# A hybrid decoder trunk: the first mixer's output projection as seven block products

## The chip, the core and the metric

The kernel runs on one core of one Trainium2 chip, in one launch. The metric is the device time of one execution in microseconds (us). A core has five engines that run their own instruction streams and wait for each other by semaphores: TensorE (PE) multiplies matrices into PSUM banks, VectorE (DVE) and GpSimd (POOL) do elementwise work, ScalarE (ACT) casts and activates, and SyncE (SP) issues the DMAs. In this kernel all DMAs of weights and activations are issued on SP's queue, in one order.

## The reference, cut to what matters

x is 1 x 1024 x 1024 (tokens by channels), float32. Layer 0 mixes by a gated delta rule (mixer A, 4 heads of 128) and a short gated convolution (mixer B, 512 channels); layer 1 has other mixers. Each mixer's outputs are concatenated and mapped by one output projection; a SwiGLU FFN follows each.

```
def mixer_ab(...):
    ...
    return jnp.concatenate([o_a, o_b], axis=-1) @ w_out          # 1024x1024 by 1024x1024

def reference(x, ...):
    h = x
    for layer in range(DEPTH):                                   # DEPTH = 2
        hn = rms_norm(h, norm_mix_g[layer])
        h = h + (mixer_ab if layer % 2 == 0 else mixer_cd)(hn, ...)
        hn = rms_norm(h, norm_ffn_g[layer])
        h = h + swiglu(hn, ffn_w_gate[layer], ffn_w_up[layer], ffn_w_down[layer])
    return rms_norm(h, norm_final_g)
```

The case is about `concat @ w_out` of layer 0, the addition to h behind it and the `rms_norm` that follows.

## The kernel before

Activations are kept transposed: channels on the 128 partitions, tokens along the free axis, in two halves of 512 tokens (`NH` = 2, `HT` = 512) and eight blocks of 128 channels (`KT` = 8, `KH` = 4). Precision is kept by splitting: `split(hi, lo, src)` lets ACT cast a float32 tile to a shorter type (L102) and DVE subtract that from it (L103), and `mm3` multiplies a 128x128 block of weights with a 128x512 block of activations by three matmuls, hi x hi, hi x lo and lo x hi (L127, L128, L129). A weight unit is one 128x1024 tile, loaded by one 512 KB DMA into `raw` (tag "raw", 2 buffers) and split into `w` (`unit()`, 4 buffers).

*The mixer's front.* `mixer_ab` opens with a loop over four heads and two halves (`for u in range(8)`, L1606). Each turn makes q, k, v and the gate z by projections on PE, runs a causal convolution over them on DVE (`xp` L1315, `cacc` L1531 and L1533), and lets `step(u, i)` work on the scalars and the chunk matrices of an earlier turn (`cx`, L1570 to L1589). POOL does little there: copies and clears of the convolution's carry (L1312, L1314, L1524), one 128x512 mask product a turn (L1589), and the power that makes an inverse root (`pow`: `power` L216 for the trunk's norm, L1559 for q and k). The norm of the second half of x is made inside the first turns: `sums` (PE L200, then DVE `rows` L204), `inverse` (PE transposes the rows, L209; DVE copies `v`, L211; POOL raises it to -1/2, L216) and `spread` (PE L240 copies the result over the partitions). `bat` (L1332, PE L1338) carries the decay and write-strength columns to the scalars `s_g` (PE L1435, L1436).

*The order.* The program's tiles and pools decide the buffers; a scheduler puts each engine's instructions in an order by priorities and a cost model, so that an instruction's place on its engine can differ from its place in the source. SP's and POOL's orders are fixed once built: what stands behind a waiting instruction waits with it.

*The output projection.* `out_proj` (L1265) runs once for each half of the tokens. It loads the eight 128x512 blocks of the concatenated mixer outputs (`cat`, in DRAM) into `cin`, splits them (`hnh`, `hnl`), and for each of eight blocks of output channels multiplies eight blocks of weights: 2 x 8 x 8 x 3 = 384 matmuls, into `psu` and `psg` banks. Each result is added to the residual tile of h by DVE (L1282); `tr.piece` squares it on ACT (L181, L184) and gathers the squares on POOL (`acc`, L188), and `tr.save` stores it to DRAM (L244). The residual itself was loaded by `tr.begin` (L168). While the second half's blocks run, the norm of the first half is made: `tr.sums` after block d = 1, `tr.inverse` after d = 2 and `norm_first` (L271) after d = 3, which spreads the norm (L240), scales eight tiles of h (DVE) and splits them. Behind it comes the FFN: `Up.turn` (L617 to L628) loads its first weights (`raw` L626, L627), makes sums of weights on POOL (`Up.sums`, L327 and L328; L617), and starts with `p1(0, b11)` and the second half's norm, `tr.sums(1)`. The FFN already uses seven block products for each of its pairs (`p1` to `p7`).

Of the kernel before, what the change touches and what calls it, by code (L numbers as in the profile page):

```python
# [9 lines left out]
F32 = mybir.dt.float32  # L10
# [8 lines left out]
P = 128  # L19
# [36 lines left out]
def hybrid_trunk_kernel(ctx: ExitStack, tc: tile.TileContext, x_t, w_all, w_down, w_ba, vecs, c_f, c_i, c_rope, out):  # L56
# [1228 lines left out]
                yield  # L1285


    def mixer_ab(hn, rb, hp, tr, first, later, second, close, wba):
        scr_n = dr.tile([4, 32, 32, 32], F32, name="scr_n")
        scr_y = dr.tile([4, 32, 32, 32], F32, name="scr_y")  # L1290
        scr_c = dr.tile([8, P, 4, CX], F32, name="scr_c")
# [99 lines left out]
        with ExitStack() as es:  # L1391
# [121 lines left out]
            if True:  # L1513
# [92 lines left out]
                for u in range(8):  # L1606
                    h, half = divmod(u, 2)
                    if half == 0:
                        wqk, wvz = first if h == 0 else (wload(("ab", h), ("ab", 4 + h)),
                                                         wload(("ab", 8 + h), ("ab", 12 + h)))  # L1610
                        carry = at("carry", (3, 3), p=fp)
                    kk = at("kq", (2, HT), 3, fp)
                    v = at("vch", p=fp)
                    conv_silu(h, 0, wk(wqk, 0), half, carry, kk[:, 1, :])
                    step(u, 0)
                    conv_silu(h, 1, wk(wqk, 1), half, carry, kk[:, 0, :])
                    step(u, 1)
                    conv_silu(h, 2, wk(wvz, 0), half, carry, v)
                    step(u, 2)
                    z_gate(h, half, wk(wvz, 1), early.pop((u, 3), None))  # L1620
                    step(u, 3)
                    waiting.append((h, half, kk, v))
            def inverses():
# [883 lines left out]
    for layer in range(2):  # L2507

        if layer == 0:
            mixer_ab(hn, rb, hp, tr, first, later, second, es.close, wba)  # L2510
# [12 lines left out]
        row = R_FFN + layer * KT  # L2523
        for half in range(NH):
            steps = out_proj(("abo", "cdo")[layer], cat[layer][half], tr, residual[half],
                             ((4, 5, 6, 7, 0, 1, 2, 3), (0, 1, 2, 4, 5, 6, 3, 7))[layer], half, hp)
            for d, _ in enumerate(steps):
# [118 lines left out]
```

## Time and profile before

| what | us |
|---|---|
| median of 3 runs | 2542.97 (2541.15 to 2545.13) |
| the profiled execution's own time | 2541.42 |
| its span | 2539.6 |
| PE busy in it | 2513.7 |
| DVE busy | 1695.1 |
| ACT busy | 1079.6 |
| POOL busy | 644.3 |

The span runs from the first to the last instruction; 1.8 us of the execution lie outside it. Times in rows of the timeline count from the span's start. A row of the timeline gives start, duration, engine, line, operation, written tile and read tiles, shape and type, count, and in brackets the idle time of the engine ahead of it with what ended that. A row of the stretches gives its bounds and length, then the busy time (and the number of instructions) of PE, PE's weight loads, DVE, ACT and POOL, the granted clock, DMA's share and GB/s. A row of the waits names the waiting engine, tile and line, the releaser, and the sum, number and longest of the waits. Rows of DMA issues end with KB and the median us to landing. Matmuls are pipelined, so a matmul's row lasts longer than the step from one start to the next.

### The profile page before, as it was taken

To read this page: it belongs to the slowest core of one execution; us is meant where nothing else is said; L and a number is where in the kernel's file an instruction comes from. 1 tells how busy PE (TensorE), PEld (TensorE's weight loads), DVE (VectorE), ACT (ScalarE), POOL (GpSimd) and SP (SyncE) were. 2 spreads that over 40 slices of the span, in tenths; PEclk is the share of its full clock that TensorE was granted. 3 is DMA by queue.
4 is the path that set the end of the run, shared out by engine and by line. 5 is a ranking of instruction groups with operands and counts; after the bars stand their busy time and mean duration, and the time that the engine had idled before them with its cause. 6 is when DMAs were issued, how large, how long until landed. Compare 5 with 4: busy or idle time off the path is not lost.

```text
span 2539.6 us, 37517 instructions
## 1 busy us (share of the span) xinstructions
PE 2513.7 (99%) x13957; PEld 2083.5 (82%) x13957; DVE 1695.1 (67%) x2857; ACT 1079.6 (43%) x1827; POOL 644.3 (25%) x557
## 2 busy tenths in 40 slices
PE   9999999999999999999999999999999999999998
PEld 7888888888888888878887889888788888888887
DVE  8887786685656565567788666567668565666554
ACT  5432113353333345334676544456535333334442
POOL 0111111343333300033566410000133333330001
PEclk9999999999999999999999999999999999999999
DMA  4435447325556688544344534576732555568753
GB/s 161 156 121 167 128 155 260 114 92 182 182 191 210 204 299 295 182 139 141 127 141 147 191 120 135 156 199 213 245 137 87 177 190 191 200 216 286 276 175 125
DMA packets 281174, 451.48 MB, mean 178 GB/s; under 512 B 49152, under 2 KB 137760, under 8 KB 280736
## 3 DMA queue, kind: packets, MB, share of 16 engines
q1 hardware_dynamic: 280992, 449.10, 53.8%
q8 instruction: 109, 1.79, 0.3%
q14 instruction: 73, 0.60, 0.1%
HBM read 304.74 MB, written 144.26 MB: 177 GB/s over the span
## 4 chain that ended last, share of the span: by engine, by line
PE 38%; DVE 5%; ACT 3%; issue 2%; POOL 1%; DMA 1%; SPq 0%; POOLq 0%; DVEq 0%; ACTq 0%
PE psu L127 7%; PE psu L129 7%; PE psu L128 7%; PE psg L127 3%; PE psg L128 3%; PE psg L129 3%; PE psm L127 2%; PE psm L129 2%; PE psm L128 2%; PE psm L2255 1%; ACT w L102 1%; DVE w L103 1%; PE psg L1985 0%; POOL sw L853 0%; DVE c L832 0%
## 5 line engine op out<-in xcount | busy, mean ns | idle before, releaser
L103 DVE TENSOR_TENSOR w<-raw,w 128x1024 fp32r<-128x1024 f32 (+1 forms) x322 | 385.1, 1198 | 122.0 <-ACT w L102 121.4
L102 ACT CAST w<-raw 128x1024 fp32r<-128x1024 f32 (+1 forms) x322 | 307.9, 958 | 267.1 <-PE psu L129 135.6
L127 PE MATMUL psu<-hnh,w 128*128 128x512 f32 x832 | 331.7, 399 | 0.5 <-ACT w L102 0.5
L129 PE MATMUL psu<-hnh,w 128*128 128x512 f32 x832 | 325.8, 392 | 0.5 <-DVE w L103 0.5
L128 PE MATMUL psu<-hnl,w 128*128 128x512 f32 x832 | 325.2, 391 | 0.0
L188 POOL TENSOR_TENSOR acc<-acc,sq 128x512 f32<-128x512 f32 x52 | 78.7, 1514 | 517.0 <-ACT sq L184 477.3
L129 PEld LDWEIGHTS psu<-hnh,w 128*128 128x128 f32 x832 | 156.6, 188 | 34.6 <-DVE w L103 0.8
L127 PEld LDWEIGHTS psu<-hnh,w 128*128 128x128 f32 x832 | 156.7, 188 | 33.0 <-ACT w L102 1.0
L128 PEld LDWEIGHTS psu<-hnl,w 128*128 128x128 f32 x832 | 156.7, 188 | 31.0
L327 POOL TENSOR_TENSOR ws<-raw 128x512 f32<-128x512 f32 x54 | 70.5, 1306 | 400.6 <-DMA raw<-in_dram 201.6
L103 DVE TENSOR_TENSOR w<-ws,w 128x1024 fp32r<-128x1024 f32 x51 | 67.1, 1317 | 117.3 <-ACT w L102 117.3
L103 DVE TENSOR_TENSOR hidq<-hr,hidq 128x1024 fp32r<-128x1024 f32 x72 | 82.1, 1141 | 78.7 <-ACT hidq L102 78.7
L102 ACT CAST hidq<-hr 128x1024 fp32r<-128x1024 f32 x72 | 70.3, 980 | 103.3 <-DMA hr<-ts 60.3
L127 PE MATMUL psm<-hidq,w 128*128 128x512 f32 (+1 forms) x275 | 106.1, 386 | 0.0
L128 PE MATMUL psm<-hidq,w 128*128 128x512 f32 (+1 forms) x275 | 105.8, 385 | 0.0
L129 PE MATMUL psm<-hidq,w 128*128 128x512 f32 (+1 forms) x275 | 105.8, 385 | 0.0
L853 POOL TENSOR_TENSOR sw<-sw,rope 128x512 f32<-128x512 f32 x48 | 71.6, 1491 | 96.0 <-ACT sw L852 62.7
L127 PE MATMUL psu<-t3h,w 128*128 128x512 f32 x240 | 93.8, 391 | 1.4 <-ACT u L390 1.4
L127 PE MATMUL psu<-t4h,w 128*128 128x512 f32 x240 | 93.7, 391 | 0.5 <-ACT c L397 0.5
L418 POOL TENSOR_TENSOR hid<-hid,c 128x512 f32<-128x512 f32 x44 | 62.0, 1410 | 126.5 <-ACT hid L417 126.4
L333 POOL TENSOR_TENSOR raw<-raw,ws 128x512 f32<-128x512 f32 x51 | 77.9, 1528 | 62.5 <-DVE w L103 62.5
L128 PE MATMUL psu<-t4l,w 128*128 128x512 f32 x240 | 93.4, 389 | 0.0
(536 smaller groups left out, 6684.1 us busy)
## 6 DMA issues: line engine op xcount, KB each, us to landing
raw<-in_dram SPq DMA_DIRECT2D x227, 512.0 KB, 4.2
sd<-in_dram SPq DMA_DIRECT2D x44, 512.0 KB, 3.9
hid<-hid SPq DMA_DIRECT2D x88, 256.0 KB, 2.9
sd<-sd SPq DMA_DIRECT2D x44, 512.0 KB, 3.3
hr<-ts SPq DMA_DIRECT2D x40, 512.0 KB, 4.4
raw<-sd SPq DMA_DIRECT2D x40, 512.0 KB, 4.6
qk<-z SPq DMA_DIRECT2D x52, 256.0 KB, 2.9
hd<-h SPq DMA_DIRECT2D x48, 256.0 KB, 2.4
```

The costliest lines, as they stand in the source:

```text
L102: S.copy(hi, src)
L103: eng.tensor_tensor(lo, src, hi.bitcast(F32), op=SUB)
L127: T.matmul(o, lh, rh, start=first and i == 0, stop=False, **kw)
L128: T.matmul(o, lh, rl, start=False, stop=False, **kw)
L129: T.matmul(o, ll, rh, start=False, stop=last and i == n - 1, **kw)
L188: (eng or G).tensor_tensor(a, a, q, op=ADD)
L327: G.tensor_tensor(s[:, HT:], b[:, :HT], b[:, HT:], op=ADD)
L333: G.tensor_tensor(a[:, HT:], a[:, HT:], s[:, :HT], op=SUB)
L418: G.tensor_tensor(h, h, self.c22.pop(f), op=MULT)
L853: G.tensor_tensor(sw, sw, self.table[:, 1, t], op=MULT)
L2255: T.matmul(po[:, jj * P:(jj + 1) * P], pt[:, z.start + i * P:z.start + (i + 1) * P], self.vp[:, j - m + 1 + i, :], start=i == 0, stop=i == ...
```

## The change

The projection of layer 0 is made over both halves of the tokens at once, as a product of 2 x 2 blocks: output channels and input channels in halves of 512, tokens in halves of 512. Seven products of 512x512 by 512x512 take the place of eight, by sums on both sides. With x = the operand's upper channels of token half 0, z its lower channels, y and w the same of token half 1:

- the operands' sums are t1 to t4, made from x, y, z, w in place: y - w (t3) and then x + y - w (t2) on DVE, z less t2 (t4) and w less t2 (t1) on POOL, two operations of 128x1024 each;
- the weights' sums are four matrices of 512x512. They are made in the mixer's front by POOL (`sums`, four 128x512 operations for each of four pairs of output blocks), from a 1 MB tile `cin` filled by two 512 KB loads (`load`), and written to DRAM by one 1 MB store into `so`; the projection reads them from there as weight units;
- the seven products run one after another, each over four blocks of output channels (`q`), on two sets of four PSUM banks, `oa` and `ob`; three of them are accumulated onto what stands in `oa`, one onto what stands in `ob`, and after each block DVE adds the bank into a tile of h (28 adds);
- the residual is loaded in four lots between the products; the first half's norm is made inside the sixth product (`tr.sums` after q = 0, `tr.inverse` after q = 1, `norm_first` after q = 2);
- PE's order within this stage is written out by hand (`manual_schedule` for PE); the other engines' orders and everything outside are the scheduler's.

In the built order the first `load` stands behind the mixer's first weight load on SP, the first `sums` follow the first three copies of the carry on POOL (in the profile of before at 29.69), the other three come between there and about 90 us. Layer 1's projection is left as it was. `quarter()` gives a 128x4x512 pair of hi and lo; `tag="m"` of `hp` was four buffers of 128x512 and is one of 128x4x512.

```
+    class Seven:
+        def __init__(self, name, hp):
+            self.name, self.hp = name, hp
+            self.sums_d = dr.tile([4, P, KH, HT], F32, name="so")
+            self.block = None
+        def place(self):
+            return self.hp.tile([P, KH, HT], F32, tag="m", name="cin", bufs=1)
+        def load(self, q):
+            a = self.place()
+            for i in range(2):
+                dma(a[:, 2 * i:2 * i + 2, :], w_all[W_AT[self.name, q + i * KH]].rearrange("p (x c) -> p x c", x=2))
+            self.block = q, a
+        def sums(self):
+            q, a = self.block
+            a12, a11, a22, a21 = (a[:, i, :] for i in range(4))
+            G.tensor_tensor(a22, a21, a22, op=ADD)
+            G.tensor_tensor(a21, a11, a21, op=SUB)
+            G.tensor_tensor(a11, a22, a11, op=SUB)
+            G.tensor_tensor(a12, a12, a11, op=SUB)
+            dma(self.sums_d[:, :, q, :].rearrange("s p n -> p s n"), a)
+        def weights(self, src):
+            us = []
+            for g in range(2):
+                t = ring.tile([P, DM], F32, tag="raw", name="raw", bufs=2)
+                if isinstance(src, int):
+                    dma(t, self.sums_d[src][:, 2 * g:2 * g + 2, :].rearrange("p i c -> p (i c)"))
+                else:
...
+                us.append(unit())
+                split(us[-1][:, 0, :], us[-1][:, 1, :], t)
+            return us
+        def run(self, cat_d, tr, src, row):
...
+            def part(o, us, b, q, first):
+                u, c = us[q // 2], q % 2 * HT
+                mm3(o, [(u[:, 0, c + k * P:c + (k + 1) * P], u[:, 1, c + k * P:c + (k + 1) * P], b[0][:, k, :],
+                         b[1][:, k, :]) for k in range(KH)], first, True, skip_group_check=True)
+            def add(half, d, o, done=False):
+                h = tr.at(half, d)
+                V.tensor_tensor(h, h, o, op=ADD)
+                if done:
+                    tr.piece(half, d, n=(d + half * KH) % KT)
+                    tr.save(half, d, hd[0][half])
+            def each(op, eng, dst, x, y):
+                for a in (0, 2):
+                    eng.tensor_tensor(dst[:, a:a + 2, :], x[:, a:a + 2, :], y[:, a:a + 2, :], op=op)
...
+                b11, b21 = quarter(), quarter()
+                splits(b11, x)
+                w1 = self.weights((0, hi))
+                operand(z, 0, lo)
+                splits(b21, z)
+                w2 = self.weights((0, lo))
+                operand(y, 1, hi)
+                operand(w, 1, lo)
...
+                w6 = self.weights(1)
+                tr.load(0, src[0], range(KH))
+                oa = [psg(), psm(), psm(), psm()]
+                ob = [psu(), psu(), psu(), psg()]
+                for q in range(4):
+                    part(oa[q], w1, b11, q, True)
+                    add(0, q, oa[q])
+                each(SUB, V, y, w, y)
+                each(ADD, V, x, y, x)
+                t2 = quarter()
+                splits(t2, x)
+                w7 = self.weights(3)
+                tr.load(1, src[1], range(KH))
+                for q in range(4):
+                    part(ob[q], w2, b21, q, True)
+                    add(0, q, ob[q], True)
+                t3 = quarter()
+                splits(t3, y)
+                each(SUB, G, z, z, x)
...
+                for q in range(4):
+                    part(oa[q], w6, t2, q, False)
+                    add(1, q, oa[q])
+                t4 = quarter()
+                splits(t4, z)
+                each(SUB, G, x, w, x)
+                w4 = self.weights((1, lo))
...
+                for q in range(4):
+                    part(oa[q], w7, t3, q, False)
+                    add(1, q + KH, oa[q])
+                t1 = quarter()
+                splits(t1, x)
+                w5 = self.weights(2)
+                for q in range(4):
+                    part(oa[q], w4, t4, q, False)
+                    add(0, q + KH, oa[q], True)
+                b22 = quarter()
+                splits(b22, w)
+                w3 = self.weights(0)
+                for q in range(4):
+                    part(ob[q], w5, t1, q, True)
+                    add(1, q + KH, ob[q], True)
+                    if q == 0:
+                        parts = tr.sums(0, ahead=60)
+                    if q == 1:
+                        dg = tr.inverse(*parts)
+                    if q == 2:
+                        first = norm_first(tr, row, dg)
+                for q in range(4):
+                    part(ob[q], w3, b22, q, False)
+                    add(1, q, ob[q], True)
+            return first
@@ mixer_ab, the loop over u
                     z_gate(h, half, wk(wvz, 1), early.pop((u, 3), None))
+                    if 2 < u < 7:
+                        seven.sums()
+                    if 1 < u < 6:
+                        seven.load(u - 2)
@@ the loop over the layers
+            seven = Seven("abo", hp)
+            mixer_ab(hn, rb, hp, tr, first, later, second, es.close, wba, seven)
...
-        for half in range(NH):
+        if layer == 0:
+            with tc.manual_schedule(engines={mybir.EngineType.PE}):
+                b1 = seven.run(cat[0], tr, residual, row)
+        for half in range(NH) if layer else ():
```

More of the change, by code (lines that the diff above doesn't have):

```diff
@@ L1289, in mixer_ab @@
+    def mixer_ab(hn, rb, hp, tr, first, later, second, close, wba, seven):
         scr_n = dr.tile([4, 32, 32, 32], F32, name="scr_n")
@@ L2509, in hybrid_trunk_kernel @@
         if layer == 0:
-            mixer_ab(hn, rb, hp, tr, first, later, second, es.close, wba)
+            seven = Seven("abo", hp)
+            mixer_ab(hn, rb, hp, tr, first, later, second, es.close, wba, seven)
         else:
```

18 lines of the change are left out of this document (17 added, 1 removed).

## The prediction

> **What bounds the kernel now.** I read the page's first two parts, then the busy time of each engine by stretches, then what TensorE (PE) waited for, then the timeline of the two stages that the change touches.
>
> ```profile
> span 2539.6 us, 37517 instructions
> PE 2513.7 (99%) x13957; PEld 2083.5 (82%) x13957; DVE 1695.1 (67%) x2857; ACT 1079.6 (43%) x1827; POOL 644.3 (25%) x557
> PEclk9999999999999999999999999999999999999999
> 0.00:60.00 60.00, 57.75 (x287) 41.65 (x288) 49.12 (x83) 33.07 (x50) 6.18 (x19) 1.00 0.46 159
> 60.00:120.00 60.00, 59.01 (x282) 49.24 (x281) 54.08 (x137) 26.40 (x83) 10.74 (x16) 1.00 0.49 157
> 400.00:520.00 120.00, 119.62 (x552) 97.88 (x552) 77.33 (x93) 46.36 (x59) 36.08 (x22) 1.00 0.52 176
> PE psg L1581 <- DVE cx L1586: 1.0, 1, 1.0
> PE psg L129 <- DVE w L314: 0.5, 1, 0.5
> ```
>
> PE is busy 99% of the span at a clock that never falls below the top digit, so a matmul taken away shortens the kernel, and a PE wait that is put in lengthens it; there is nearly no idle time that could swallow one. The stretches (columns: PE, PE loads, DVE, ACT, POOL) show two different surroundings: in the first 120 us VectorE (DVE) is at 82% and 90%, so it has 11 and 6 us of slack and nothing more; in the 120 us round the output projection it has 43. The waits say how near the front already is to DVE: its longest, after the start, is a DVE one.
>
> **What goes: 48 matmuls.**
>
> ```profile
> 408.38 0.40 PE L127 MATMUL psu<-hnh,w 128*128 128x512 f32 x1
> 494.81 0.39 PE L128 MATMUL psg<-hnl,w 128*128 128x512 f32 x1
> 496.40 0.39 PE L129 MATMUL psg<-hnh,w 128*128 128x512 f32 x1
> 496.63 0.39 PE L127 MATMUL psu<-hnh,w 128*128 128x512 f32 x1
> ```
>
> The old projection starts at 408.38 and the FFN's first product at 496.63: 88.2 us for 2 x 8 x 8 x 3 = 384 matmuls and a few small ones. Seven starts lie between 494.81 and 496.40, so one matmul is 1.59/7 = 0.227 us. The new stage has 7 x 4 x 4 x 3 = 336: 48 x 0.227 = **-10.9 us**. The order of PE's instructions really is 48 shorter, so that the change misses its aim altogether is excluded.
>
> **What comes in the front.** Sixteen POOL sums (128x512), eight 512 KB loads and four 1 MB stores. In the source they stand late in the head loop, but in the changed order of POOL the first four follow the carry copy of 29.69 and three of the second block stand ahead of the `pow` of 44.15. On SP each store stands, waiting for its block's last sum, ahead of weight loads; the next two loads, into the same buffer, wait for that store's landing. Rows for this chain:
>
> ```profile
> 29.69 0.19 POOL L1524 COPY carry<-xp 128x3 f32<-128x3 f32 x1 [0.41 <-DVE xp L1315]
> 44.15 1.46 POOL L216 TENSOR_TENSOR r<-v,mhalf 128x4 f32<-128x4 f32 x1
> L188 POOL TENSOR_TENSOR acc<-acc,sq 128x512 f32<-128x512 f32 x52 | 78.7, 1514 | 517.0 <-ACT sq L184 477.3
> scr_c<-cx SPq DMA_DIRECT2D x8, 1216.0 KB, 4.8
> raw<-in_dram SPq DMA_DIRECT2D x227, 512.0 KB, 4.2
> 26.61 0.69 DVE L1315 TENSOR_TENSOR xp<-psu,rb 128x512 f32<-128x512 f32 x1 [0.32 <-ACT rb L1373]
> ...
> 42.92 0.29 DVE L204 TENSOR_SCALAR rows<-psm 128x128 f32<-128x128 f32 x1 [0.66 <-PE psm L200]
> 48.50 0.60 PE L240 MATMUL psm<-cf,r 128*128 128x128 f32 x4
> 50.92 0.68 DVE L1332 TENSOR_TENSOR bat<-psg,rb 128x512 f32<-128x512 f32 x1
> 51.68 0.70 PE L1338 MATMUL psm<-cf,bat 128*128 128x8 f32 x5
> ```
>
> Does a POOL sum cost DVE anything? These rows say yes:
>
> ```profile
> 108.15 0.68 DVE L1315 TENSOR_TENSOR xp<-psu,rb 128x512 f32<-128x512 f32 x1
> 108.37 1.29 POOL L1589 TENSOR_TENSOR cx<-cx,masks 128x512 f32<-128x512 f32 x1 [3.63 <-issue]
> 108.75 1.99 DVE L103 TENSOR_TENSOR w<-raw,w 128x1024 fp32r<-128x1024 f32 x1
> 46.52 1.21 DVE L103 TENSOR_TENSOR w<-raw,w 128x1024 fp32r<-128x1024 f32 x1
> 131.65 1.67 POOL L1589 TENSOR_TENSOR cx<-cx,masks 128x512 f32<-128x512 f32 x1 [3.16 <-DVE cx L1586]
> 132.09 1.91 DVE L1570 SCALAR_TENSOR_TENSOR dm<-bc,s_gc,masks 128x128 f32<-128x128 f32 x3
> 513.44 5.25 POOL L617 TENSOR_TENSOR raw<-xa,raw 128x512 f32<-128x512 f32 x1 [9.23 <-DMA raw<-in_dram]
> 512.91 2.35 DVE L617 TENSOR_TENSOR t1l<-h,t1h 128x1024 fp32r<-128x1024 f32 x2
> ```
>
> The DVE split took 1.21 us at 46.52, but 1.99 at 108.75 beside a POOL operation that ran to 109.66: it lost 0.78. The three small ones at 132.09 met a POOL operation that had 1.23 to run, so lost at most that. The PSUM reader at 108.15 was not slowed. And at 513.44 the loser is POOL: 5.25 us for a 1.3 us operation while DVE streams two-input operations. So a sum costs DVE between 0 and 1.29, mostly about **0.8**, and itself takes 1.3 to 5.3.
>
> [...]
>
> Chain, with 1.51 us a sum (the L188 mean): the first four run 29.9 to 36.0, the store lands at 41, the next loads at 46, three sums end at 50.5, the `pow` at 52.0, where PE wants its result at 48.50: **+3.5**. By then DVE has lost 7 x 0.8 = 5.6, less about 1 of idle time (0.66 at 42.92 and another such gap): `bat` ends 4.6 later and PE at 51.68 with it, **+4.5 in all, not on top**. The two other blocks take 8 x 0.8 = 6.4 from DVE between about 60 and 90 us, of which I let 2.4 go into its gaps (6 us in that whole stretch): +4. Front: **+8.5**. Low end: half the sums fall beside PSUM readers or gaps, 3. High end: every sum costs its 1.29, 20.6 - 4 = 16.6. The value is the row's mean, since DVE's work here is mixed. The weight loads behind the stores come some 3 us later than before, which the PE delay by then covers; without that cover they would cost those 3.
>
> **What comes in the projection's stage.** Twelve more DVE adds into h (28, not 16), four DVE and four POOL operations of 128x1024 for the operands; fourteen 128x1024 operand splits for 32 of 128x512; 14 weight splits for 16; six 512 KB loads for sixteen of 256 KB. DVE: 12 x 0.68 + 4 x 1.2 + 14 x 1.2 - 32 x 0.68 - 2 x 1.2 = +5.6 us, covered by the 43 of slack over the stage, but not everywhere:
>
> ```profile
> 410.21 0.33 SPq L1508 DMA_DIRECT2D cat<-obt  x1
> 410.11 0.68 DVE L103 TENSOR_TENSOR hnl<-cin,hnh 128x512 fp32r<-128x512 f32 x1
> 469.88 1.02 POOL L216 TENSOR_TENSOR r<-v,mhalf 128x4 f32<-128x4 f32 x1 [3.41 <-DVE v L211]
> 488.00 0.33 SPq L627 DMA_DIRECT2D raw<-in_dram  x1
> 491.60 1.30 POOL L327 TENSOR_TENSOR ws<-raw 128x512 f32<-128x512 f32 x1 [2.51 <-DMA raw<-in_dram]
> 492.97 2.15 POOL L328 TENSOR_TENSOR ws<-ws,raw 128x512 f32<-128x512 f32 x1
> ```
>
> *The third product's operand.* It starts at 408.38 + 96 x 0.227 = 430.2 and needs y - w, x + y and two splits. Everything waits for the last `cat` write (410.21, so landed near 413); the six loads come in by about 423 (an estimate: 3 MB behind it and between weights). Then 4 x 1.2 + 2 x 1.2 = 7.2 us of DVE, and in the same 7 us two adds (1.4) and a weight split (1.2): 432.8 for the second half, wanted at 431.6 (its first half covers six matmuls): +1.2. The four POOL subtractions of 128x1024 (2 x 1.3 each) fall near: if two stand before it, +5.2. I take **+1.5**, bounds 0 and 6.
>
> *The spread of the first half's norm.* It now has the rest of the sixth product and its transpose as cover instead of two pairs of the projection. In the changed order the `pow` (469.88 before, with POOL free) stands behind two weight sums of the FFN (L327, L328: before at 491.60, 20 us later than it), which wait for a weight load, which waits for a split behind the fifth product's end S. S + 3.2 for the issue (an ACT and a DVE split, 1 + 1.2, and the queue), + 3.6 landing (issued at 488.00, it let L327 go at 491.60), + 1.3 + 2.15 + 1.02 = S + 11.3; PE wants it after three parts of 12 matmuls and the small ones, S + 9.0. **+2.2**, bounds 0.5 and 4.
>
> *The tail.* The norm's eight scales and splits now share 13.6 us (five parts) with nine adds, where before they had four pairs of 5.45; DVE may carry up to 2 us of debt into the FFN's turn, where PE already waits 0.5 for a DVE operation. **+0.5**, bounds 0 and 1.5. The moved residual loads are asked for earlier than their adds by a product or more (10.9 us): nothing; if SP held them, that product would wait.
>
> **Sum.** -10.9 + 8.5 + 1.5 + 2.2 + 0.5 = +1.8 on the profiled execution of 2541.42 (span 2539.6 and 1.8 round it): 2543.2. That execution lies 1.55 below the median of the runs, 2542.97, so as a median I forecast **2545**: the gain is eaten, mostly by the sums. Ends: -10.9 + 3 + 0.5 = -7.4, or 2535.6; -10.9 + 16.6 + 6 + 4 + 1.5 = +17.2, or 2560.
>
> **The rivals.**
> *The sums are hidden (faster).* POOL is busy 6 and 11 us in the first two stretches of 60, so it has room; DVE has 17 us of slack there against 12.8. If the scheduler's place lets the sums meet PSUM readers and gaps, the front costs 1 to 3 and the total is -10.9 + 2 + 2.7 = -6, about **2537**, and 2534 if the spread is in time as well. Against it: DVE has no gap between the xp of 26.61 and the rows of 42.92 (nothing idle before any row between them), where the first four fall.
> *POOL starves (slower).* DVE streams two-input operations from 30 to 42 without a gap; if each of the first sums takes the 5.25 of 513.44, four end at 51, the store at 56, the next loads at 61 and the `pow` after three more at 66 to 70: PE would stand some 17 us at the spread instead of 3.5, of which DVE then uses part to catch up. It decides as soon as the first four take over 3 us each on average. -10.9 + 17 + 4 = +10: **2553**.
> *The third operand decides (slower in part).* Both POOL pairs fall ahead of it: +6 there with the rest as forecast, 2549.5, just over the bound.
> [...]
>
> **Chances.** 0.2% (5 us, about what can be told here from no change) bounds "same" at 2538 to 2548. Forecast 0.42, hidden 0.25, starved 0.25, third operand 0.08. The forecast's own spread crosses the upper bound in some 0.04, and of the third operand's case 0.02 stay below it: faster 0.25, same 0.42 - 0.04 + 0.02 = 0.40, slower 0.35. Range 2534 to 2558: it takes in the hidden case whole and the starved one up to its middle third; cut off are its far end and a front that costs nothing with an undisturbed stage.
>
> **What would show it.** Right: PE's waits in the first 100 us grow by some 8 us, named L240, L1338, L1435 and released by POOL `r` and DVE; the new POOL group at 1.3 to 1.7 us, and DVE's groups beside it (L1533, L103, L188) with longer means; between 408 and the FFN 48 fewer matmuls and about 82 us in place of 88; an L240 wait on POOL `r` before the seventh product. Wrong: PE waits in the front unchanged (hidden), a POOL sum mean above 3 us (starved), or a wait of more than 3 us at the third product. If the stage itself is no shorter than 86 us, the stage was mis-costed rather than the front.

## The result: 0.8% slower, and where it went

The changed kernel took 2562.96 us (median of 4 runs, 2561.23 to 2565.81) where the kernel before took 2542.06 in the same series: a ratio of 1.0081, 95% interval 1.0064 to 1.0099. Its profiled execution took 2563.78 with a span of 2562.0, so 22.4 us more span than before. First the page of the changed kernel (busy times), then its stretches with the columns of before: PE, PE's loads, DVE, ACT, POOL, granted clock, DMA.

```profile
span 2562.0 us, 37469 instructions
PE 2517.1 (98%) x13917; PEld 2084.0 (81%) x13917; DVE 1727.9 (67%) x2869; ACT 1082.2 (42%) x1823; POOL 685.4 (27%) x576
```

```profile
0.00:60.00 60.00, 52.14 (x254) 36.38 (x254) 50.31 (x70) 30.39 (x46) 18.95 (x25) 0.98 0.63 214
60.00:120.00 60.00, 54.71 (x238) 44.58 (x238) 53.57 (x116) 22.45 (x77) 21.70 (x23) 0.90 0.54 181
400.00:520.00 120.00, 110.47 (x513) 90.31 (x511) 92.42 (x115) 46.52 (x54) 42.62 (x23) 0.96 0.54 187
```

PE was busy 57.75, 59.01 and 119.62 us in these stretches before; it has lost 5.6, 4.3 and 9.2. But the granted clock has fallen too (0.98, 0.90 and 0.96 in place of 1.00), which the page's second part does not show: its slices are 64 us long and a 9 stands for 90% or more. PE's busy time rose by 3 us over the span although 48 matmuls are gone: matmuls at half clock count as busy for about twice as long (0.43 us from start to start in place of 0.23, rows below).

PE's own rows in the timeline (brackets: idle before, and what ended it) give all waits over 0.5 us from the start's own to the FFN:

```profile
43.61 0.43 PE L200 MATMUL psm<-acc,onesn 128*32 128x128 f32 x8 [1.23 <-DVE acc L188]
46.71 0.33 PE L209 MATMUL psm<-cf,rows 128*128 128x128 f32 x1 [1.56 <-DVE rows L204]
52.47 0.65 PE L240 MATMUL psm<-cf,r 128*128 128x128 f32 x4 [0.64 <-POOL r L216]
58.35 1.88 PE L1474 MATMUL psm<-cf,bat 128*128 128x8 f32 x8 [2.46 <-DVE bat L1468]
85.95 0.38 PE L1571 MATMUL psm<-s_g,masks 128*128 128x32 f32 x2 [2.32 <-issue]
103.12 2.07 PE L1717 MATMUL psg<-kq 128*128 128x256 f32 x4 [2.65 <-DVE cx L1722]
448.10 0.50 PE L128 MATMUL psg<-hnl,w 128*128 128x512 f32 x1 [1.25 <-DVE hnl L103]
454.71 0.80 PE L128 MATMUL psg<-hnl,w 128*128 128x512 f32 x1 [4.96 <-DVE hnl L103]
500.70 0.65 PE L240 MATMUL psm<-cf,r 128*128 128x128 f32 x4 [2.61 <-POOL r L216]
521.51 0.43 PE L200 MATMUL psm<-acc,onesn 128*32 128x128 f32 x8 [2.22 <-POOL acc L188]
```

A point that the forecast had no term for shows in the same timeline right after the wait at 58.35:

```profile
60.65 0.63 PE L128 MATMUL psu<-hnl,w 128*128 128x512 f32 x1
61.08 0.63 PE L129 MATMUL psu<-hnh,w 128*128 128x512 f32 x1
...
64.91 0.39 PE L129 MATMUL psu<-hnh,w 128*128 128x512 f32 x1
65.14 0.40 PE L127 MATMUL psu<-hnh,w 128*128 128x512 f32 x1
```

The matmuls start 0.43 us apart (60.65, 61.08), and only from 64.91 on 0.23 again. The stretches of single microseconds show it as the clock (third column from the right):

```profile
59.00:60.00 1.00, 1.00 (x6) 1.00 (x6) 1.00 (x3) 0.00 (x0) 0.00 (x0) 0.50 0.98 391
63.00:64.00 1.00, 1.00 (x3) 0.78 (x3) 1.00 (x2) 0.00 (x0) 0.10 (x1) 0.50 0.99 397
65.00:66.00 1.00, 1.00 (x6) 0.83 (x5) 0.00 (x0) 0.66 (x1) 0.00 (x0) 1.00 0.52 209
```

I added up, over the stretches of 1 us as far as the FFN's first turn, PE's busy time by (1 - clock): the time that half clock cost. It is 3.3 us at 58 to 65, 3.1 at 102 to 110, 3.1 at 454 to 461, and 1.7 each at 501 to 506 and 522 to 526, each time from the end of one of the waits above on; in the kernel before it is nothing in the same stages. With it the 22.4 us nearly close:

| term | us |
|---|---|
| 48 matmuls less | -10.9 |
| waits in the front, 11.2 (with one of 0.33) against 1.4 before | +9.8 |
| half clock in the front | +6.3 |
| waits in the projection's stage: 1.25 + 4.96 + 2.61 + 2.22 | +11.0 |
| half clock in the stage | +6.5 |
| sum | +22.7 |

In between, the last transpose that closes the mixer (L1831 before, L1971 after) comes at 407.6 before and 423.9 after: +16.3 for the front. This "mixer's end" and "the rest" (span less mixer's end: 2132.0 before, 2138.1 after) serve as the two measures below.

### The profile page after: what moved, and what is told of

The parts are those of the page before. It is cut to its first block, busy times and chain, and to the rows that moved or that the text cites. A ratio compares the mean times of both kernels' runs of the same rounds, so it can differ in the third digit from the quotient of the medians.

```text
span 2562.0 us, 37469 instructions
## 1 busy us (share of the span) xinstructions
PE 2517.1 (98%) x13917; PEld 2084.0 (81%) x13917; DVE 1727.9 (67%) x2869; ACT 1082.2 (42%) x1823; POOL 685.4 (27%) x576
## 4 chain that ended last, share of the span: by engine, by line
PE 82%; DVE 9%; ACT 3%; issue 2%; DMA 2%; POOL 1%; SPq 0%; POOLq 0%; DVEq 0%; ACTq 0%
PE psu L127 15%; PE psu L129 15%; PE psu L128 15%; PE psg L127 5%; PE psg L129 5%; PE psg L128 5%; PE psm L127 5%; PE psm L129 5%; PE psm L128 5%; DVE w L103 1%; PE psm L2395 1%; DVE w L314 1%; PE psg L1717 1%; DVE h L250 1%; DVE h L617 1%
## 5 line engine op out<-in xcount | busy, mean ns | idle before, releaser
L103 DVE TENSOR_TENSOR w<-raw,w 128x1024 fp32r<-128x1024 f32 (+1 forms) x320 | 382.1, 1196 | 120.2 <-ACT w L102 119.5
L127 PE MATMUL psu<-hnh,w 128*128 128x512 f32 x804 | 322.7, 401 | 0.9 <-ACT w L102 0.9
L129 PE MATMUL psu<-hnh,w 128*128 128x512 f32 x804 | 316.3, 393 | 0.5 <-DVE w L103 0.5
L128 PE MATMUL psu<-hnl,w 128*128 128x512 f32 x804 | 315.4, 392 | 0.0
L188 POOL TENSOR_TENSOR acc<-acc,sq 128x512 f32<-128x512 f32 x51 | 79.9, 1566 | 481.2 <-ACT sq L184 480.7
L129 PEld LDWEIGHTS psu<-hnh,w 128*128 128x128 f32 x804 | 152.3, 189 | 33.9 <-DVE w L103 0.8
L127 PEld LDWEIGHTS psu<-hnh,w 128*128 128x128 f32 x804 | 152.4, 190 | 32.8 <-ACT w L102 1.3
L327 POOL TENSOR_TENSOR ws<-raw 128x512 f32<-128x512 f32 x54 | 70.8, 1311 | 402.7 <-DMA raw<-in_dram 272.9
L103 DVE TENSOR_TENSOR w<-ws,w 128x1024 fp32r<-128x1024 f32 x51 | 66.9, 1312 | 118.0 <-ACT w L102 118.0
L103 DVE TENSOR_TENSOR hidq<-hr,hidq 128x1024 fp32r<-128x1024 f32 x72 | 82.1, 1141 | 78.5 <-ACT hidq L102 78.5
L127 PE MATMUL psm<-hnh,w 128*128 128x512 f32 x264 | 103.4, 392 | 0.0
L128 PE MATMUL psm<-hnl,w 128*128 128x512 f32 x264 | 103.4, 392 | 0.0
L129 PE MATMUL psm<-hnh,w 128*128 128x512 f32 x264 | 103.4, 392 | 0.0
```

What stands on the lines that cost most here:

```text
L103: eng.tensor_tensor(lo, src, hi.bitcast(F32), op=SUB)
L127: T.matmul(o, lh, rh, start=first and i == 0, stop=False, **kw)
L128: T.matmul(o, lh, rl, start=False, stop=False, **kw)
L129: T.matmul(o, ll, rh, start=False, stop=last and i == n - 1, **kw)
L188: (eng or G).tensor_tensor(a, a, q, op=ADD)
L327: G.tensor_tensor(s[:, HT:], b[:, :HT], b[:, HT:], op=ADD)
```

## The experiments

e1 to e10 rest on one execution each, and single executions of the kernel before ran from 2539.3 to 2547.5 us; so these runs are read by the mixer's end and by named waits, and a difference of 3 us between two of their spans says little. From e11 on a ratio rests on nine or ten executions beside 18 or 19 of the kernel before.

### What the front alone costs, and the stage alone (e1, e2)

e1 adds to the kernel before the class's `load` and `sums` and their calls (and makes four `cin` buffers one, as the change does), nothing else; e2, whose edit is shown, takes them from the changed kernel and lets it read plain weight blocks in place of the sums.

```
-                    if 2 < u < 7:
-                        seven.sums()
-                    if 1 < u < 6:
-                        seven.load(u - 2)
...
-                if isinstance(src, int):
-                    dma(t, self.sums_d[src][:, 2 * g:2 * g + 2, :].rearrange("p i c -> p (i c)"))
-                else:
-                    m, ks = src
+                if 1:
+                    m, ks = ((0, lo), (0, hi), (1, lo), (1, hi))[src] if isinstance(src, int) else src
```

> The kernel before, with the loads, the 16 POOL sums and the stores added to its front at the same places as in the changed kernel, and nothing made of them. Theory (the front alone costs what I read from the change's trace: seven PE waits of 11.2 us against 1.4 before, and two stretches at half clock worth 6.3): the last L1831-type transpose of the mixer, at 407.6 before and 423.9 after, comes at 423 to 425, and the span is 2539.6 + 16.8 = about 2556. Rival (part of the 16.8 comes from the rest of the reordering that the new projection brings): the mixer ends below 416 and the span below 2549.

> The changed kernel without the front's loads, sums and stores; the projection takes unsummed blocks of the weights in the place of the four sums, so the projection's output is left wrong by that, with the same loads and splits. Theory: the mixer ends within 1 us of before (407.6), the stage keeps its three waits (6.2 at the third operand, 2.6 at the spread, 2.2 at the second half's sums) and three half-clock stretches, so 2562.0 - 16.3 = about 2546 of span. Rival (the stage's waits are inherited from a front that left DVE, SP or the ring of weights late): the third operand's wait is below 2 us and the span below 2540.

e1: span 2561.0, mixer's end 425.9 (of it 1.7 a wait of its own, at 425.5). The same waits stand at the same places: 0.9, 1.6, 0.6, 2.5, 2.3, 3.2 us, and half clock costs 3.2 and 3.1. The span is 5 us over what was expected; 3.3 of them are the 1.7 and a stretch at half clock near 1850 that costs 3.3 here and 1.7 before, the rest I cannot name. e2: span 2544.3, mixer's end 407.2, no half clock in the front, and the stage's waits nearly as they were: 0.87 (1.25 in the changed kernel), 4.96, 2.63, 2.22. So front and stage are two separate losses; the rival of inherited waits falls.

### Why the front costs it (e3, e10)

The lines view, grouped by shape, over the same work (28 to 91 us before, 28 to 103 after) says what POOL's sums did to DVE. Columns: count, busy, mean ns. Before, then after:

```profile
L1533 DVE SCALAR_TENSOR_TENSOR cacc<-xp,vec,cacc 128x512 f32<-128x512 f32 x27 | 19.6, 743 | 0.1
L1315 DVE TENSOR_TENSOR xp<-psu,rb 128x512 f32<-128x512 f32 x8 | 5.3, 684 | 0.9 <-PE psu L129 0.9
L1537 DVE SCALAR_TENSOR_TENSOR kq<-cth,cacc 128x512 f32<-128x512 f32 x6 | 4.1, 688 | 0.0
L2420 DVE SCALAR_TENSOR_TENSOR hnl<-h,vec,hnh 128x512 fp32r<-128x512 f32 x4 | 2.7, 746 | 0.0
```

```profile
L1669 DVE SCALAR_TENSOR_TENSOR cacc<-xp,vec,cacc 128x512 f32<-128x512 f32 x27 | 23.5, 886 | 0.1
L1673 DVE SCALAR_TENSOR_TENSOR kq<-cth,cacc 128x512 f32<-128x512 f32 x6 | 6.2, 1048 | 2.6 <-ACT cth L1671 2.6
L2560 DVE SCALAR_TENSOR_TENSOR hnl<-h,vec,hnh 128x512 fp32r<-128x512 f32 x4 | 5.9, 1524 | 0.0
L1451 DVE TENSOR_TENSOR xp<-psu,rb 128x512 f32<-128x512 f32 x8 | 5.3, 680 | 0.0
```

Two-input operations on SBUF grew (`cacc` 743 to 886 ns, `kq` 688 to 1048, `hnl` 746 to 1524), the one that reads a PSUM bank (`xp<-psu`, 684 and 680) did not. Over these and three more groups (L103 1218 to 1453 ns, four; L188 688 to 859, six; the scalar multiply L1667 471 to 687, nine) DVE lost 3.9 + 2.1 + 3.2 + 0.9 + 1.0 + 1.9 = 13.0 us: 0.8 for each of the 16 sums. Three tiny scalar operations (128x32; 1.26, 1.04 and 0.86 us in place of 0.16 to 0.18) add 2.7, which makes it 1.0. e3 puts clears in the sums' place, which only write; e10 leaves the sums and takes the stores from SP's queue.

```
-            G.tensor_tensor(a22, a21, a22, op=ADD)
...
+            for x in (a22, a21, a11, a12):
+                for _ in range(3):
+                    G.memset(x, 0.5)
```

```
-            dma(self.sums_d[:, :, q, :].rearrange("s p n -> p s n"), a)
+            G.dma_start(out=self.sums_d[:, :, q, :].rearrange("s p n -> p s n"), in_=a)
```

> The changed kernel, each POOL sum in the front replaced by three clears of the same tile (0.53 us each, so 1.6 as the sums took); loads, stores and POOL's and SP's orders stay; the weights' sums are left out by this. Theory A (POOL's reads of SBUF shut out DVE's two-input operations, and DVE is what PE waits for): the four hnl operations at 30.1 fall from 5.86 to about 2.7, the front's waits of 11.2 fall below 4, and the span comes to 2562 - 10 or more: 2548 to 2552. Rival B (what costs is the order: the pow behind the sums on POOL, the weight loads behind the stores on SP): DVE's rows get short but the waits at L240, L1474, L1571 and L1717 stay near 8 us and the span above 2557.

> The changed kernel with the four stores on POOL's own queue. Theory (in the front the cost is mostly DVE shut out by POOL's reads, as e3 shows, and SP's queue the smaller part): the front's waits of 11.2 fall by 2 to 5 only, mixer's end at 417 to 423, span 2555 to 2561. Rival (SP's queue is the cause here too): mixer's end below 414, span below 2552.

e3: span 2551.6, mixer's end 412.9 (11.0 us earlier); e10: 2559.1 and 422.7 (1.2 earlier). So 11.0 of the front's 16.3 us go when POOL only writes the tile in place of reading it too, and SP's queue is a small part; the 5.3 that e3 keeps (its waits of 4.4 are just over the mark of 4) were not taken apart. In e3 (timeline of DVE and POOL) the two-input operations run at their old length, but for one split, and something else now suffers:

```profile
30.67 2.73 DVE L2559 SCALAR_TENSOR_TENSOR hnl<-h,vec,hnh 128x512 fp32r<-128x512 f32 x4
49.47 2.16 DVE L1597 TENSOR_SCALAR zs<-zs 128x512 f32<-128x512 f32 x1
62.44 4.24 DVE L1549 TENSOR_SCALAR bt<-bt 128x32 f32<-128x32 f32 x1
62.53 4.15 DVE L103 TENSOR_TENSOR w<-raw,w 128x1024 fp32r<-128x1024 f32 x1
49.42 1.93 POOL L1311 MEMSET cin<- 128x512 f32 x4
60.99 5.65 POOL L1311 MEMSET cin<- 128x512 f32 x12 [1.51 <-DMA cin<-in_dram]
```

A scalar multiply of 0.43 us (L1462 before) takes 2.16 beside the clears, and a tiny scalar addition of 0.17 (L1414 before) takes 4.24: it lasts until the run of clears has ended. The split right behind it (62.53, 1.2 us elsewhere) ended with it; the profile does not say which of the two was held. The waits that are left in e3 (1.05 at `bat`, 1.61 at `s_g`, 1.77 at `cx`) stand where the changed kernel has them, at `bat` and `cx` for DVE; at `s_g` the profile names no releaser. The four `hnl` operations take 5.9 us in the changed kernel, where POOL's sums read SBUF, and 2.73 in e3, where its clears only write; but the scalar operations above grew beside writes alone, and no trace here shows why.

### The third operand (e4)

```
-                each(SUB, G, z, z, x)
+                each(SUB, V, z, z, x)
...
-                each(SUB, G, x, w, x)
+                each(SUB, V, x, w, x)
```

> The changed kernel with the four 128x1024 operand subtractions on DVE in place of POOL. Theory A (each POOL subtraction, 3.2 us, holds a DVE split for 2.1 us more, and two of them stand ahead of the third operand's last split): the wait of 6.2 us at the third product falls to 0 to 2, its half-clock stretch (3.1 us) goes, span 2562 - 6 to -9 = 2553 to 2556. Rival B (the operands land too late: y and w at about 439.7, and the chain behind them is long without POOL too): the wait stays above 4 us and the span above 2558.

Span 2553.0, mixer's end 422.9, the rest 2130.1 in place of 2138.1. Before and after the edit, timeline of DVE and POOL, changed kernel first, then e4:

```profile
446.82 1.22 DVE L103 TENSOR_TENSOR hnl<-cin,hnh 128x1024 fp32r<-128x1024 f32 x1
447.96 3.41 DVE L103 TENSOR_TENSOR w<-raw,w 128x1024 fp32r<-128x1024 f32 x1
451.30 3.35 DVE L103 TENSOR_TENSOR hnl<-cin,hnh 128x1024 fp32r<-128x1024 f32 x1
447.04 3.25 POOL L1354 TENSOR_TENSOR c<-c,cin 128x1024 f32<-128x1024 f32 x1 [1.39 <-ACT hnh L102]
450.25 3.32 POOL L1354 TENSOR_TENSOR cin<-c,cin 128x1024 f32<-128x1024 f32 x1
```

```profile
445.89 1.22 DVE L103 TENSOR_TENSOR hnl<-cin,hnh 128x1024 fp32r<-128x1024 f32 x1
447.03 1.22 DVE L103 TENSOR_TENSOR w<-raw,w 128x1024 fp32r<-128x1024 f32 x1
448.16 1.22 DVE L103 TENSOR_TENSOR hnl<-cin,hnh 128x1024 fp32r<-128x1024 f32 x1
452.83 4.28 DVE L103 TENSOR_TENSOR hnl<-c,hnh 128x1024 fp32r<-128x1024 f32 x2
460.40 0.67 DVE L1347 TENSOR_TENSOR h<-h,psg 128x512 f32<-128x512 f32 x1
```

Each POOL subtraction made the DVE split beside it 2.2 us longer, and the split that PE waits for stood behind two of them: 1.25 + 4.96 became 1.26 + 0.60, and the half clock after it went. In its place the fourth product waits 2.11 us for the add of 460.40: DVE is full there, and two splits (4.28 in place of 2.4) ran beside three gathers of squares on POOL. The waits at the spread and the sums of the second half became 0.2 and 2.57. The first of these is an order that changed with the edit: the scheduler now put the norm's `pow` (490.34) ahead of the FFN's weight sum (L327, 493.65), where the changed kernel has it behind two of them (496.16, 497.53, `pow` 499.62). So not all of e4's gain belongs to the third operand.

### Where the sums could stand (e5 to e9, e11 to e16)

All of these have e4's edit; from e7 and e8 on also the `pow` of the first half's norm ahead of the FFN's weight sums on POOL (a higher priority; e4's order had it there already) and the last product's squares gathered on DVE; e9 and later also the stores on POOL's own queue; from e12 on the second product's squares on DVE too. e5 and e7 load one block in each of the turns u = 3 to 6, held back by a small copy that reads the turn's v, and sum it a turn later; e6 and e8 put all after the turns. The cut is e5's.

```
+            G.tensor_copy(a[:, :, 0:1], gate[:, 0:4, None])
...
-                    if 2 < u < 7:
+                    if 3 < u < 8:
                         seven.sums()
-                    if 1 < u < 6:
-                        seven.load(u - 2)
+                    if 2 < u < 7:
+                        seven.load(u - 3, v)
```

> The kernel of e4 (operand subtractions on DVE), and the front's sums spread: one block in each of the turns u = 3 to 6, each load held back by a small POOL copy that reads that turn's v, so that nothing stands in the first 120 us. Theory (the sums cost what DVE loses and cannot make up before PE wants it; from 125 us on DVE has 1 to 3 us idle in each 10 and PE waited only 0.4 there): the mixer ends at 407.6 to 411 in place of 422.9, span 2553.0 - 12 to -16 = 2537 to 2541. Rival (the sums cost their 16 x 0.8 us wherever they stand): the mixer ends above 417.

> The kernel of e4 with all 16 sums after the last turn, behind the clear of the substitution's tile (at about 246 us), where POOL then is idle until 296 but DVE is at 93 to 98% with the substitution's chain. Theory (DVE's share decides, not POOL's): this place costs more than e5, as the substitution is late by up to 16 x 0.8 = 13 us and PE waits at the first products that need it: mixer's end 412 to 420, span 2542 to 2550. Rival (the 31-step chain has slack before PE needs it, PE has other products to do): the end at 407 to 410 and a span like e5's or less.

> e5, and the pow of the first half's norm ahead of the FFN's weight sums on POOL, and the last product's four squares gathered on DVE in place of POOL. Theory (the spread's wait comes from POOL's order, the second half's sums' wait from POOL's four slow gathers, 7.6 us, beside DVE): both waits fall below 1 us and their half-clock stretches with them: e5 - 3 to -6. Rival (the pow's own input is late, or the DVE gathers only move the wait onto DVE's queue): e5 - 1 to +1, with the waits named after DVE.

> e6 with the same two edits as e7. Theory: the same gain against e6 as e7 has against e5, to within a half-clock stretch of 1.7 us. Rival: the two places of the sums change what stands round the stage, and the gains differ by more than 3.4 us.

e5: span 2553.9, mixer's end 423.0, no better than the front: the theory missed and the rival's mark (an end above 417) was met; PE waited 4.3 us at 176 and 4.3 at 228 and lost 4.8 to half clock. e6: 2559.1 and 428.7, worst of all, with waits of 10.3 at 278 and 8 at 304; but its own copies stood in the substitution's way (DVE waited for one), so it says little on the place. e7 against e5 gains 3.2 us, e8 against e6 1.3. What both share is the wait at the second half's sums, which falls from 2.6 to 0.7; that at the spread stays at 0.2. Of e7's gain 1.7 is a half-clock stretch near 1660 that e5 has and e7 has not, and e8's mixer ended 1.7 later than e6's.

In e5 the weight loads behind the stores on SP were 10 us late (159.26 in place of 149.09), so I took SP's queue for the cause; e9 tests it.

> e7 with the four stores issued on POOL's own queue behind its sums, in place of SP's. In e5 and e7 the waits of 4.3 (at 176) and 4.1 us (at 228) follow weight loads that SP issued 10 and 8 us later than before, each right behind such a store. Theory (in the spread place the cost is SP's queue, not DVE's lost time): both waits and their half-clock stretches (1.7 + 3.2) go, the mixer ends at 408 to 412 in place of 422.9, span 2550.7 - 11 to -15 = 2536 to 2540. Rival (DVE's lost 12.8 us come back as waits wherever the sums stand): the mixer still ends above 417.

It fell: span 2553.9, mixer's end 426.5, waits of 4.6 and 5.6. What really stood behind the sums shows in e9's timeline of POOL and DVE:

```profile
153.95 1.29 POOL L1310 TENSOR_TENSOR cin<-cin 128x512 f32<-128x512 f32 x1 [5.92 <-DMA cin<-in_dram]
158.40 1.29 POOL L1313 TENSOR_TENSOR cin<-cin 128x512 f32<-128x512 f32 x1
160.85 1.69 POOL L1697 TENSOR_TENSOR r<-n,mhalf 128x8 f32<-128x8 f32 x1
155.71 1.26 DVE L1695 TENSOR_SCALAR n<-n 128x8 f32<-128x8 f32 x1
162.57 0.17 DVE L1699 COPY s_rk<-r 128x4 f32<-128x4 f32 x1 [5.59 <-POOL r L1697]
```

`n` is ready at 157, but its `pow` waits on POOL until four sums, which had themselves waited for their load, are through; DVE idles 5.6 us for it (1.75 before) and is that much late from there on. e11 holds the load back until the `pow` is done and puts the sums of three blocks behind the mask product, of the fourth behind the clear of the substitution's tile; e12 adds the edit on the squares.

```
                     G.tensor_tensor(r8, n8, mhalf[:, 0:8], op=ALU.pow)
+                    at_ = {2: 0, 4: 1, 6: 2, 7: 3}.get(2 * h + half)
+                    if at_ is not None:
+                        seven.load(at_, r8)
...
                     G.tensor_tensor(qk, qk, tri[:, None, :].to_broadcast([P, 4, P]), op=MULT)
+                    if at_ is not None and at_ < 3:
+                        seven.sums()
```

> e9 with each block's load held back until the pow of a half's q and k is done, and its sums right behind the mask product that ends that half's chunk matrices (in three halves; the fourth block's behind the clear of the substitution's tile). In e5 and e9 the pow of q and k stood behind four sums on POOL, DVE idled 5.6 us for it and PE waited 4.6 (at 178) and 5.6 us (at 232). Theory (in the spread place the cost was POOL's order: a sum that waits for its load keeps the pow behind it): DVE's idle time ahead of s_rk is 2 us again as before, the mixer ends at 408 to 413 in place of 426.5, span 2537 to 2542, so faster than the kernel before by 0 to 6 us. Rival (DVE's lost 12.8 us come back wherever the sums stand): the mixer's end stays above 417 and the span above 2545.

> e11, with the squares of the second product's four tiles gathered on DVE too. In e7 POOL's three gathers at 451 to 458 ran beside two DVE splits that took 4.28 us in place of 2.4 and two subtractions of 3.44 in place of 2.4, and PE waited 2.1 us at the fourth product. Theory (three gathers of 0.68 on DVE cost it less than three of 1.3 to 1.9 on POOL): that wait falls below 1.2, 1 to 3 us faster than e11. Rival (DVE is the bound there and gets work more): the wait grows, same as e11 or 1 to 2 us slower.

> e12 with the first block moved out of the crowded place at 110 (there PE waited 4.5 us at 126.6 in e11 and e12): two blocks stay behind mask products (at about 160 and 210), the third behind the clear of the substitution's tile (in e11 the block there, 241 to 248, had no PE wait after it), and the fourth right behind it (about 257 to 264). Theory (the sums' price is their place: 6 us in a crowded one, 1.4 to 3 beside the turns, nothing at 241): PE's waits before 300 fall from 8.5 to 3 or 4.5, the mixer ends at 411 to 414, span 2538 to 2541, ratio to before 0.997 to 0.999. Rival (the substitution's chain of two-input operations is delayed by two blocks until PE waits for it, as in e6 near 280 and 304): waits above 4 us between 265 and 310, span above 2545.

> e13 with the fourth block in the recurrence instead: its load held back by the first chunk's pow (about 320) and its sums behind the second chunk's. Theory (POOL is free there and DVE at 80%): mixer's end within 1.5 us of e13's, span 2538 to 2541. Rival (the recurrence is one chain through DVE and POOL, so 4 x 0.8 us there go straight to the end): mixer's end 3 us or more later than e13's.

> e13 with all four blocks one behind the other from the clear of the substitution's tile on (about 225, 242, 258 and 275), none beside the turns. Theory (there only the substitution's DVE chain is slowed, and PE has other products to do until about 292): the waits of e13 at 174, 221 and 225 (4.2 us) go, but the chain of 31 steps is 4 to 8 us later and PE waits for yd at 292 up to 5 us: mixer's end 409 to 414, span 2537 to 2542. Rival (with four blocks the chain comes 10 us late or more, as in e6, or the weight loads behind the block loads on SP do): span above 2545.

> e13 with the block of 210 moved behind the fourth: one block at about 160, three from about 236 on. Theory: the waits at 221 and 225 (2.8 and, with the ACT one, 3.2 us) go, the wait for yd at 292 grows from 1.1 by at most 3: mixer's end 411 to 415, span 2538 to 2543, no more than 2 us from e15. Rival: as for e15, span above 2545.

| run | blocks stand at about | PE waits over 1 us, 100 to 360 us | mixer's end | span | ratio to before, interval |
|---|---|---|---|---|---|
| before | - | none | 407.6 | 2539.6 | |
| e11 | 110, 164, 218, 242 | 4.5, 1.4, 1.5, 1.3 | 418.3 | 2547.2 | 1.0013 (1.0003 to 1.0023) |
| e12 | as e11 | 4.6, 1.4, 1.4, 1.0 | 419.2 | 2545.4 | 1.0010 (1.0001 to 1.0020) |
| e13 | 160, 210, two from 236 | 1.4, 1.5, 1.3, 1.1 | 414.4 | 2542.0 | 1.0000 (0.9990 to 1.0009) |
| e14 | 160, 210, 236, recurrence | 1.4, 1.4, 1.0, 3.1 | 419.9 | 2546.4 | 1.0015 (1.0006 to 1.0025) |
| e15 | four from 230 | 4.0, 4.8, 1.5 | 421.5 | 2546.9 | 1.0028 (1.0018 to 1.0037) |
| e16 | 160, three from 230 | 1.4, 1.2, 3.9 | 415.6 | 2540.1 | 1.0005 (0.9995 to 1.0014) |

The spans are of one execution; e15's and e16's lie at the low ends of theirs (2546.9 to 2550.8, 2540.0 to 2545.1), so the ratios rank better. e11 confirms the POOL order: DVE's idle time ahead of `s_rk` is 1.8 to 1.9 us again, and the mixer ends 8 us earlier than in e9. But that is not the size expected, and the rival's marks (417, 2545) were met too: the first block fell where DVE was busy 18.4 of 19 us already (108 to 127 before), and PE waited 4.5. e12's edit brought the wait at the fourth product from 2.1 to 0.9; the medians, 2547.8 and 2545.57, were measured side by side. e13 missed its own marks narrowly (414.4 and 2542.0). e14's rival was right: in the recurrence one block costs 3.1 us of wait and 3.4 of half clock. e15 came out at the rival's side. e16 ended near the theory's bounds, but 6.8 us and not 2 from e15 in span, and by another wait than it named: 3.9 us at 275 for `gct`, none over 0.3 for `yd`. So the price is partly place, but no place was free: wherever the four blocks went, the mixer ended at least 6.8 us later than before.

No version beats the kernel before. e13 equals it (2543.68 against 2543.69), and e16, whose profiled span was the shortest, cannot be told from it either.

### What the stage is worth once repaired

"The rest" carries a half-clock stretch near 1830 to 1850 that has nothing to do with the change and costs 0 to 3.3 us from run to run (e5 and e10 have one near 1660). Without it the rest is 2130.3 us before, 2136.5 in the changed kernel, 2127.0 in e4, 2126.1 in e7, 2124.5 in e12, 2124.4 in e13 and 2124.5 in e16. The seven products, repaired, gain 5.8 us of the 10.9; the remaining waits at products three, four and at the norms (e13: 1.1, 0.6, 0.9, 0.7, 0.7) are most of the other 5.

## Why the forecast was wrong, step by step

*48 matmuls, -10.9:* right in number. e2 and the stage's waits agree with it: 2138.1 - 11.0 - 6.5 = 2120.6 against 2132.0 is -11.4.

*The front, +8.5 of waits:* right in its main cause and nearly in size: 9.8, from DVE's loss of 13.0 us, or 15.7 with the tiny scalar operations (forecast 12.8). e3 and e10 showed that POOL's reads are the main cause and the store's place on SP a small one. The parts fit less well than the sum, and that is partly luck: the chain put 3.5 at the spread for POOL's order, where 0.64 came, while 1.2 and 1.6 came ahead of it for DVE's `acc` and `rows`, which it left out. `bat` 2.5, `s_g` 2.3 and `cx` 2.7 stand where it had put them. With these waits the hidden case falls. POOL did not starve either: its 16 sums took 1.35 to 1.61 us in the mean of their four lines.

*The third operand, +1.5 (0 to 6):* mis-sized, 6.2, what the rival of that name put there (+6), though by another way. The term counted a POOL subtraction of 128x1024 (1.3 x 2) only where it stands ahead of the operand. It took 3.2 to 3.3, and running beside DVE it cost each split 2.2; without it (e4) 1.9 of wait are left. The forecast had the price of this contention from its own rows for the front, and did not use it here.

*The spread, +2.2:* 2.61, by the order that it named: with the `pow` ahead of the weight sums (e4) the wait is 0.2.

*The tail, +0.5:* 2.2, at a place it did not name: `sums(1)` waited for POOL's gathers, four in 7.6 us beside DVE. On DVE (e7) the wait is 0.7.

*The sum is the step that failed.* It added waits at their own length ("a PE wait that is put in lengthens it"). The four terms above come to 9.8 + 6.2 + 2.6 + 2.2 = 20.8 of wait against the 12.7 that it had, and with them alone the profiled execution would have come to 2541.4 - 10.9 + 20.8 = 2551.3, inside the range. The missing term is the clock, 12.8 us: five of the seven longest waits left PE at half clock for some 3.4 to 6.6 us after them. The forecast read "never falls below the top digit" from slices of 64 us, in which a dip of 3 us cannot show. Stretches of 1 us of the kernel before have one:

```profile
1826.41 0.49 PE L127 MATMUL psg<-hnh,w 128*128 128x512 f32 x1 [1.79 <-ACT w L102]
1828.77 0.63 PE L127 MATMUL psu<-hnh,w 128*128 128x512 f32 x1
1829.20 0.63 PE L128 MATMUL psu<-hnl,w 128*128 128x512 f32 x1
```

```profile
1828.00:1829.00 1.00, 1.00 (x4) 0.81 (x3) 1.00 (x1) 0.00 (x0) 0.92 (x2) 0.50 0.45 61
```

A wait of 1.8 us (behind one of 0.55) and then 0.43 us from matmul to matmul for 3.4 us, 1.7 us lost. That row was there to be found, and it would have put a price of about 1.7 us on an added wait of such a length.

Of the marks that it gave: the waits of the front by 8 us, the POOL group at 1.3 to 1.7, the longer DVE means and the L240 wait on POOL `r` were all there. So were two that it gave as signs of being wrong: a wait of more than 3 us at the third product (4.96), and a stage of over 86 us, "mis-costed" (92.5, from 423.88 to 516.41).

## What to carry to other kernels

On a kernel bound by PE, price an added wait at its length and, from about 2 us on, at 1.4 to 3.3 us more that the clock may cost (here it did after all 22 waits of 3 us or more and after 14 of the 25 between 2 and 3); look for dips of the clock in stretches of 1 us, not in the page's slices. Work put on an idle POOL is not free when DVE is nearly full: here each 128x512 sum took 0.8 to 1.0 us from DVE, each 128x1024 subtraction 2.2, more than the 1.2 that DVE itself needs for it. Before POOL is given work that waits for a load, look for what small operation on DVE's path (here a `pow`, for which DVE idled 5.6 us in e9, 1.75 before) will stand behind it.

## What the runs showed of the hardware

*What a wait does to the clock depends on more than its length.* The changed kernel and e4 have the same front. In both PE waits about 1.2 us near 43.6 and 1.56 near 46.7. The stretch of 47 to 48 us, in the changed kernel and then in e4:

```profile
47.00:48.00 1.00, 1.00 (x6) 0.82 (x5) 1.00 (x1) 0.00 (x0) 0.92 (x2) 1.00 0.00 0
```

```profile
47.00:48.00 1.00, 1.00 (x4) 0.81 (x4) 1.00 (x1) 0.00 (x0) 0.92 (x2) 0.50 0.00 0
```

The same waits cost 1.5 us of clock in e4 and nothing in the changed kernel. In the same way the wait of 2.32 us at 85.95 in the changed kernel, and one of 2.57 at 512.1 in e4, left the clock at 1.00, while waits of 2.22 to 2.65 elsewhere lost 1.7 to 3.3. In all the traces of this case, between 20 and 560 us, half clock followed each of the 22 waits of 3 us or more and 14 of the 25 between 2 and 3; it cost 1.4 to 3.3 us each time. Many of these are the same wait in kernels that share most of their code. In the changed kernel the half-clock stretches last about 3.4 us or nearly twice that (1.7 us lost at a clock of 0.50, or 3.1 to 3.3).

No trace here shows why equal waits fare differently. Nor does a wait have to be long: one of 2.22 us (521.51 in the changed kernel) was followed by 1.7 us lost, and in e4 even the two of 1.2 and 1.56 us, with 1.5 us of matmuls between them, by 1.5.

*A run of writes alone can hold up DVE too.* POOL's clears left all two-input operations but one split at their length (the four `hnl` 2.73 us, 2.7 before), but a scalar multiply of 0.43 us took 2.16 beside them, and a tiny scalar addition 4.24, until the last clear had ended (e3).
